# Two PSUM banks of 240 and 280 columns, and one 480-column matmul for the high and the low parts

## The chip, the cores and the metric

The kernel runs on one core of one Trainium2 chip. The metric is the device time of one execution in microseconds (us), given as the median of several runs.

## What is computed

One inference step of a one-layer causal decoder trunk for 512 prompt tokens and 8 sample tokens, D_MODEL 1024, all in float32:

```
z  = rmsnorm(x) @ w_in                       # 1024 x 6656
a_in, b_x, b_gate, c_uv, gates = split(z)
ya = multiscale_pool(a_in)                   # windows 2/4/8/16, per-group 128x128 linear
yb = gelu(b_gate) * rg_lru(conv4(b_x))       # recurrence over the tokens, two 128x128 gates per head
yc = chunk_mlp(gelu(c_uv))                   # rmsnorm(v), triangular mixing in chunks of 128
merged = ga*(ya @ w_pa) + gb*(yb @ w_pb) + gc*(yc @ w_pc)
x  = x + merged @ w_o
x  = x + (gelu(conv3(rmsnorm(x) @ wg)) * (rmsnorm(x) @ wu)) @ wd      # D_FF 3072
y  = final rmsnorm(x)
```

The new states of the pool, the convolutions and the recurrence are outputs too.

## The kernel before

Features lie on the 128 partitions and the 520 tokens along the free axis, so every activation is a set of 128 x 520 tiles. To keep float32 precision with single-pass matmuls, each weight and each activation is split into a high part (rounded to fp32r) and a low part (the rest, also fp32r). The product is wh\*xh + wh\*xl + wl\*xh. For activations `hilo`, `hilos` and `hilo_scaled` (L258 to L277) do this: ScalarE writes the high part, VectorE the low one. For weights `Chunk.high` (L106, ScalarE) and `Chunk.low` (L112, VectorE) do it for each chunk of 128 x 1024 that SP's DMA queue has loaded.

An output tile is a job: 128 output features by 520 tokens, summed over k tiles of 128 input features. Its sums lie in a PSUM tile of two banks, columns 0 to 259 of the tokens in one and 260 to 519 in the other (`TH` = 260). `mm` (L118 to L123) issues six matmuls of 260 columns for each k tile, and each brings its own weight load:

```
ops = ((w[0], x[0]), (w[0], x[1]), (w[1], x[0]))
for n, (ww, xx) in enumerate(ops):
    for h in halves:
        te.matmul(ps[:, h, :TH], ww, xx[:, h * TH:(h + 1) * TH], ...)
```

The jobs have 1184 such k steps in all: 52 tiles of the input projection by 8, 8 each of w_pa and w_pc by 4, 8 each of w_pb and w_o by 8, 24 each of wg and wu by 8, and 16 of wd by 12. `lru` (16 products) and the pool linear (4) call `mm` outside the jobs.

`run_jobs` (L156 to L183) writes the order of all engines by hand. Ahead of a job's matmuls it issues the loads, high parts (`HLEAD` 3) and low parts (`LLEAD` 2) of later chunks. After them comes the job's `post`, which takes the sums from PSUM (on ScalarE for a gelu, a sigmoid or a copy; on VectorE for a product or a sum), and then whatever work was put off to that point (`after`, `chain`). So VectorE's queue holds, for each job: its post, work put off, and the low part of the weight chunk needed two jobs later. There are four PSUM tiles of two banks.

Activations sit in 61 slots (`NA`) of 536 columns. The input `xT` holds 8 of them to the end, since `x1 = xT` is the residual.

At the end, the last two tiles of wd are run half by half, so that the final norm of tokens 0 to 259 (`sums(0)`, `last(0)`) overlaps the matmuls of the other half.

Of the kernel before, what the change touches and what calls it, by code (L numbers as in the profile page):

```python
# [16 lines left out]
P = 128  # L17
# [4 lines left out]
TH = T // 2  # L22
# [24 lines left out]
# columns of the packed states: h0 (j b), conv (j r b), ffn (m r b), pool (g b r)  # L47
# [5 lines left out]
def trunk_kernel(ctx: ExitStack, tc: tile.TileContext, t: dict, o: dict):  # L53
# [9 lines left out]
    def A(name, dt=F32, w=T):  # L63
        return ap_.tile([P, 536], dt, name=name, tag="a", bufs=NA)[:, :w]
# [4 lines left out]
    def acc(ps):  # L69
        return ps[:, :, :TH]  # L70

    def two(x):
        return x.rearrange("p (h c) -> p h c", h=2)
# [4 lines left out]
    # ------------------------------------------------------------------ loads  # L78
# [11 lines left out]
    # ------------------------------------------------------------------ weight chunks  # L90
# [27 lines left out]
    def mm(ps, w, x, first, last, halves=(0, 1)):  # L118
        ops = ((w[0], x[0]), (w[0], x[1]), (w[1], x[0]))
        for n, (ww, xx) in enumerate(ops):  # L120
            for h in halves:
                te.matmul(ps[:, h, :TH], ww, xx[:, h * TH:(h + 1) * TH],  # L122
                          start=first and n == 0, stop=last and n == 2)  # L123
# [26 lines left out]
    def job(parts, post, pre=None, halves=(0, 1), mid=None):  # L150
        """An output tile: parts [(chunk, tile of the chunk, moving operands by k)], and
        post(psum) that takes the sums off; mid = (k, fn) runs fn before that k"""
        jobs.append((parts, post, pre, halves, mid))
        for c, _, _ in parts:
            if c not in order:
                order.append(c)  # L156

    def run_jobs():
        ahead = [(LOADS, "raw", Chunk.load), (HLEAD, "h", Chunk.high), (LLEAD, "l", Chunk.low)]
        at = [0] * 3  # L160
        for n0 in [0, *range(2, len(jobs))]:
# [12 lines left out]
            for n, each in enumerate(zip(*ops)):
                for (c, a, X, k), ps, (_, _, _, halves, mid) in zip(each, pss, group):
                    if mid and mid[0] == n:
                        mid[1]()
                    mm(ps, c.w(k, a), X(k), n == 0, n == len(ops[0]) - 1, halves)
            for ps, each, (_, post, _, halves, _) in zip(pss, ops, group):
                now[0] += len(each) / 8 * len(halves) / 2  # L180
                post(ps)
                run_later(now[0] + 1e-6)
# [8 lines left out]
    # ------------------------------------------------------------------ constants  # L191
# [20 lines left out]
    # state parts of the sample tokens' convolutions  # L212
# [12 lines left out]
    def constants():  # L225
# [8 lines left out]
        # old rows of the sample states  # L234
# [4 lines left out]
    # 4 softplus(-lambda) = 4 (max(-lambda, 0) + log1p(exp(-|lambda|)))  # L239
# [18 lines left out]
    # ------------------------------------------------------------------ helpers  # L258
    def hilo(x, name):
        h, l = A(name + "h", F32R), A(name + "l", F32R)  # L260
        s.activation(h, x, AF.Copy)
        v.tensor_sub(l, x, f(h))
        return h, l

    def hilos(xs, names):
        r = [(A(n + "h", F32R), A(n + "l", F32R)) for n in names]
        for x, (h, _) in zip(xs, r):
            s.activation(h, x, AF.Copy)
        for x, (h, l) in zip(xs, r):
            v.tensor_sub(l, x, f(h))  # L270
        return r

    def hilo_scaled(x, sc_, name):
        h, l = A(name + "h", F32R), A(name + "l", F32R)
        s.activation(h, x, AF.Copy, scale=sc_)
        v.scalar_tensor_tensor(l, x, sc_, f(h), op0=ALU.mult, op1=ALU.subtract)
        return h, l  # L277
# [37 lines left out]
    def rstd_psum(r, name):  # L315
        """[m, n] to all partitions, along the tokens"""
        r, m, tot = r
        ps = PS(name + "b")
        for i, dg in enumerate(r):
            for h in range(tot // TH):  # L320
                te.matmul(ps[:, h, :TH], onesr[:m, :], dg[:, h * TH:(h + 1) * TH], start=i == 0, stop=i == 1)
        return ps

    def rstd_bcast(r, name):
        out = A(name + "r")
        s.activation(two(out), acc(rstd_psum(r, name)), AF.Copy)
# [18 lines left out]
    # ------------------------------------------------------------------ branch B: conv, RG-LRU  # L345
    hs = [None] * 8

    def lru(j, ext):
# [20 lines left out]
        def gates():  # L369
            for n, off in (("r", 0), ("i", 8)):  # L370
# [3 lines left out]
                s.activation(two(y), acc(ps), AF.Sigmoid, bias=pc("bx" if off else "ba", j))  # L374
# [11 lines left out]
        def recip0():  # L386
            v.reciprocal(d["q"][:, :TH], d["q"][:, :TH])

        def recip1():
            v.reciprocal(d["q"][:, TH:], d["q"][:, TH:])  # L390
# [29 lines left out]
    def bx_raw(j, ps):  # L420
        ext = A(f"bx{j}", w=3 + T)
        g.memset(ext[:, :3], 0.0)
        s.activation(two(ext[:, 3:]), acc(ps), AF.Copy)
        held[j] = ext

    def bx_post(j, ps=None):
# [3 lines left out]
        else:  # L430
            ext = A(f"bx{j}", w=3 + T)
            g.memset(ext[:, :3], 0.0)
            v.tensor_mul(two(ext[:, 3:]), acc(ps), two(rs1[0]))
# [26 lines left out]
    # ------------------------------------------------------------------ branch A: pooling  # L460
# [4 lines left out]
    def pool_post(gi, ps):  # L465
# [4 lines left out]
        s.activation(two(a[:, 15:]), acc(ps), AF.Copy)  # L470
# [26 lines left out]
        def out():  # L497
            ps = PS("po")
            mm(ps, c_pw.w(gi), pd[gi], True, True)
            h, l = A(f"ya{gi}h", F32R), A(f"ya{gi}l", F32R)  # L500
            s.activation(two(h), acc(ps), AF.Copy, scale=pc("psc", gi))
            v.scalar_tensor_tensor(two(l), acc(ps), pc("psc", gi), two(f(h)), op0=ALU.mult, op1=ALU.subtract)
            ya[gi] = (h, l)
# [13 lines left out]
    # ------------------------------------------------------------------ gates and merges  # L517
    def gate_jobs(i0, js, gt):
        for j in js:
            def post(ps, j=j):  # L520
                y = A("gt")
                s.activation(two(y), acc(ps), AF.Sigmoid)
# [3 lines left out]
    def merge_jobs(c, i, X, gt, first):  # L526
        for a in range(2):
            def post(ps, j=2 * i + a):
                y = gt.pop(j)
                v.tensor_mul(two(y), acc(ps), two(y))  # L530
# [18 lines left out]
    # ------------------------------------------------------------------ branch C: chunked gating  # L549
# [7 lines left out]
    def v_post(k, ps):  # L557
        vt[k] = A(f"v{k}")
        s.activation(two(vt[k]), acc(ps), AF.Gelu_apprx_tanh)
# [28 lines left out]
    def u_post(k, ps):  # L588
        us[k] = A(f"u{k}")
        s.activation(two(us[k]), acc(ps), AF.Gelu_apprx_tanh)  # L590
# [18 lines left out]
    # ------------------------------------------------------------------ branch B: gate, merge  # L609
# [4 lines left out]
    def bg_post(j, ps):  # L614
        y = A(f"bg{j}")
        s.activation(two(y), acc(ps), AF.Gelu_apprx_tanh)
# [12 lines left out]
    for j in range(8):  # L629
        job([(Chunk(t["w_pb"][j], KD), 0, lambda k: yb[k])], lambda ps, j=j: pb_post(j, ps))  # L630

    # ------------------------------------------------------------------ output projection, norm 2
    xg2 = [None] * 8
    x1 = xT
    st2 = [None]

    def wo_post(j, ps):
        v.tensor_add(two(x1[j]), acc(ps), two(x1[j]))
# [6 lines left out]
    # ------------------------------------------------------------------ channel mixer  # L645
# [5 lines left out]
    def fg_post(m, ps):  # L651
        ext = A(f"fg{m}", w=2 + T)
        g.memset(ext[:, :2], 0.0)
        if rs2[0] is None:
            s.activation(two(ext[:, 2:]), acc(ps), AF.Copy)
            return ext
        v.tensor_mul(two(ext[:, 2:]), acc(ps), two(rs2[0]))
# [29 lines left out]
    def u2_post(m, ps):  # L687
        y = fy.pop(m)
        v.tensor_mul(two(y), acc(ps), two(y))
        hh[m] = hilo(y, f"h{m}_")  # L690

    def dn_post(p, j, ps, halves):
        if len(halves) == 2:
            v.tensor_add(two(x1[j]), acc(ps), two(x1[j]))  # L694
# [7 lines left out]
        c = slice(h * TH, h * TH + TH)  # L702
        v.tensor_add(x1[j][:, c], ps[:, h, :TH], x1[j][:, c])  # L703
# [9 lines left out]
    def sums(h):  # L713
        return rstd_small([st3[0], st3[1]], D, f"n3{h}", h * TH, 4, TH // 4)

    def last(h, r):
        ps = rstd_psum(r, f"n3{h}")
        c = slice(h * TH, h * TH + TH)
        for i, (j0, n) in enumerate(YG):
            y = A(f"y{h}{j0}", w=n * TH).rearrange("p (n c) -> p n c", n=n)  # L720
            for j in range(j0, j0 + n):
                v.scalar_tensor_tensor(y[:, j - j0, :], x1[j][:, c], pc("gf", j), ps[:, 0, :TH],  # L722
# [31 lines left out]
    for k in range(KD):  # L754
        h, l = A(f"xg{k}_h", F32R), A(f"xg{k}_l", F32R)
        s.activation(h, xT[k], AF.Copy, scale=pc("g1", k))  # L756
# [3 lines left out]
        v.scalar_tensor_tensor(l, xT[k], pc("g1", k), f(h), op0=ALU.mult, op1=ALU.subtract)  # L760
# [3 lines left out]
        xg.append((h, l))  # L764
# [5 lines left out]
NA, RAW, HS, LS, LOADS, HLEAD, LLEAD = 61, 4, 5, 4, 3, 3, 2  # L770
# [14 lines left out]
def _layout(w):  # L785
    """The inputs as the launch takes them: the same numbers, laid out by partition."""
# [6 lines left out]
    def cols(a, nk, cw):  # L793
        # (nk * 128, n * cw) -> (n, 128, nk * cw)
# [72 lines left out]
```

## Time and profile before

| | |
|---|---|
| median of 3 runs | 896.65 us (896.6, 896.65, 896.99) |
| span of the profiled execution | 895.0 us |
| PE busy | 884.0 us, 99% |
| VectorE (DVE) busy | 525.2 us, 59% |
| ScalarE (ACT) busy | 344.0 us, 38% |
| HBM read | 82.6 MB |

The span runs from the first to the last instruction of the profiled execution and is 1.65 us under the median of the runs, which also hold what lies around it. PEld is TensorE's weight loads, which overlap the matmuls. Starts in the trace are measured; ends of matmuls are modelled, so distances between starts are what to read.

### The profile page before, as it was taken

How to read it: one execution, taken by the hardware profiler on the slowest of the kernel's cores; microseconds unless marked ns; L12 is line 12 of the kernel's file. 1: busy time of each engine (PE TensorE's matmuls, PEld its weight loads, DVE VectorE, ACT ScalarE, POOL GpSimd, SP SyncE). 2: the span in 40 equal slices, each digit the busy share in tenths (PEclk: the TensorE clock that was granted, in tenths of full speed). 3: DMA queues.
4: the chain of work that ended last, by engine and by line, in shares of the span. 5: the costliest groups of instructions: out<-in, count | busy, mean ns of one | idle time of the engine just before them, and what ended most of it. 6: DMA issues, size and time to landing. Idle time of an engine off the chain costs nothing.

```text
span 895.0 us, 16824 instructions
## 1 busy us (share of the span) xinstructions
PE 884.0 (99%) x7358; PEld 880.8 (98%) x7358; DVE 525.2 (59%) x779; ACT 344.0 (38%) x456; POOL 56.1 (6%) x93
## 2 busy tenths in 40 slices
PE   9999999999999999999999999999999999999995
PEld 8999999999999999999999999999999999999995
DVE  5897998689665442155555666653234555554345
ACT  7554573776342342222334433332122333333210
POOL 1403311111100000000000000000000000000000
PEclk9999999999999999999999999999999999999998
DMA  9423233133232223222321422222332223323212
GB/s 293 152 99 107 73 106 98 57 96 95 72 118 72 94 92 122 71 72 95 95 94 48 131 89 90 88 71 90 106 113 77 95 94 94 95 71 116 74 37 96
DMA packets 28298, 86.12 MB, mean 96 GB/s; under 512 B 3112, under 2 KB 6312, under 8 KB 28200
## 3 DMA queue, kind: packets, MB, share of 16 engines
q1 hardware_dynamic: 26752, 83.21, 29.1%
q10 hardware_dynamic: 1376, 1.44, 0.5%
q8 instruction: 58, 0.95, 0.4%
q0 software_dynamic: 96, 0.39, 0.1%
q14 instruction: 16, 0.13, 0.0%
HBM read 82.63 MB, written 2.79 MB: 95 GB/s over the span
## 4 chain that ended last, share of the span: by engine, by line
PE 98%; DVE 1%; DMA 0%; ACT 0%; issue 0%; DVEq 0%
PE pj L122 95%; PE lru L122 1%; DVE y L722 1%; PE vm L581 0%; DMA par<-in_par 0%; PE po L122 0%; PE vt L574 0%; PE n30p L293 0%; DVE x2q L705 0%; DVE x L703 0%; PE n1p L293 0%; PE nvp L293 0%; PE n2p L293 0%; ACT xg_h L756 0%; PE n31p L293 0%; DVE n L309 0%
## 5 line engine op out<-in xcount | busy, mean ns | idle before, releaser
L112 DVE TENSOR_TENSOR wl<-raw,wh 128x1024 fp32r<-128x1024 f32 (+2 forms) x162 | 182.4, 1136 | 32.5 <-ACT wh L106 32.2
L106 ACT ACTIVATE wh<-raw 128x1024 fp32r<-128x1024 f32 (+2 forms) x162 | 156.7, 975 | 58.5 <-PE pj L122 55.5
L122 PE MATMUL pj<-x_h,wh 128*128 128x260 f32 x768 | 154.6, 283 | 0.0
L122 PE MATMUL pj<-x_h,wl 128*128 128x260 f32 x768 | 154.3, 282 | 0.0
L122 PE MATMUL pj<-x_l,wh 128*128 128x260 f32 x768 | 154.3, 282 | 0.0
L122 PE MATMUL pj<-xn_h,wh 128*128 128x260 f32 x704 | 142.1, 283 | 0.0
L122 PE MATMUL pj<-xn_l,wh 128*128 128x260 f32 x704 | 141.8, 283 | 0.0
L122 PE MATMUL pj<-xn_h,wl 128*128 128x260 f32 x704 | 141.5, 282 | 0.0
L122 PEld LDWEIGHTS pj<-x_h,wl 128*128 128x128 f32 x768 | 118.5, 188 | 0.0
L122 PEld LDWEIGHTS pj<-x_l,wh 128*128 128x128 f32 x768 | 118.1, 188 | 0.0
L122 PEld LDWEIGHTS pj<-x_h,wh 128*128 128x128 f32 x768 | 117.9, 188 | 0.0
L122 PEld LDWEIGHTS pj<-xn_h,wl 128*128 128x128 f32 x704 | 108.5, 188 | 0.0
L122 PEld LDWEIGHTS pj<-xn_h,wh 128*128 128x128 f32 x704 | 108.4, 189 | 0.0
L122 PEld LDWEIGHTS pj<-xn_l,wh 128*128 128x128 f32 x704 | 108.3, 188 | 0.0
L122 PE MATMUL pj<-h_h,wl 128*128 128x260 f32 x384 | 81.3, 283 | 0.0
L122 PE MATMUL pj<-h_h,wh 128*128 128x260 f32 x384 | 81.3, 283 | 0.0
L122 PE MATMUL pj<-h_l,wh 128*128 128x260 f32 x384 | 81.1, 282 | 0.0
L122 PEld LDWEIGHTS pj<-h_h,wl 128*128 128x128 f32 x384 | 60.9, 188 | 0.0
L122 PEld LDWEIGHTS pj<-h_l,wh 128*128 128x128 f32 x384 | 60.8, 188 | 0.0
L122 PEld LDWEIGHTS pj<-h_h,wh 128*128 128x128 f32 x384 | 60.8, 188 | 0.0
L694 DVE TENSOR_TENSOR x<-pj,x 128x520 f32<-128x520 f32 x14 | 9.8, 699 | 77.2 <-PE pj L122 77.2
L665 DVE SCALAR_TENSOR_TENSOR fc<-fg,par,fc 128x512 f32<-128x512 f32 x48 | 36.1, 752 | 18.9 <-ACT fc L663 18.0
(277 smaller groups left out, 1208.7 us busy)
## 6 DMA issues: line engine op xcount, KB each, us to landing
raw<-in_w_in SPq DMA_DIRECT2D x50, 512.0 KB, 3.6
raw<-in_wg SPq DMA_DIRECT2D x24, 512.0 KB, 3.5
raw<-in_wu SPq DMA_DIRECT2D x24, 512.0 KB, 3.5
raw<-in_wd SPq DMA_DIRECT2D x32, 384.0 KB, 3.1
raw<-in_w_pb SPq DMA_DIRECT2D x8, 512.0 KB, 3.5
raw<-in_w_o SPq DMA_DIRECT2D x8, 512.0 KB, 3.6
x<-in_x SPq DMA_DIRECT2D x8, 260.0 KB, 4.6
raw<-in_w_pa SPq DMA_DIRECT2D x4, 512.0 KB, 3.4
```

The source lines that it names most:

```text
L106: s.activation(self.h[:, q], self.raw[:, q], AF.Copy)
L112: v.tensor_sub(self.l[:, q], self.raw[:, q], f(self.h[:, q]))
L122: te.matmul(ps[:, h, :TH], ww, xx[:, h * TH:(h + 1) * TH], start=first and n == 0, stop=last and n == 2)
L665: v.scalar_tensor_tensor(y[:, :SEQ], ext[:, r:r + SEQ], pc("fcw", r * MF + m), y[:, :SEQ], op0=ALU.mult, op1=ALU.add)
L694: v.tensor_add(two(x1[j]), acc(ps), two(x1[j]))
L722: v.scalar_tensor_tensor(y[:, j - j0, :], x1[j][:, c], pc("gf", j), ps[:, 0, :TH], op0=ALU.mult, op1=ALU.mult)
```

## The change

The tokens are cut into 240 (part A) and 280 (part B). The PSUM tile is still two banks: part A ends at the end of bank 0, part B starts at bank 1, so the 520 sums lie side by side. The moving operand of each part is one slot with the low part ahead of the high part (`PAIR`). In a job, for part A, wh is multiplied with both at once: one matmul of 480 columns, whose low half lands in the 240 columns of bank 0 ahead of A's sums. A k step of a job is then five matmuls: 480 (wh; xl and xh of A), 280 (wh, xh of B), 280 (wh, xl of B), 240 (wl, xh of A), 280 (wl, xh of B). Outside the jobs (`lru`, pool) there are still six, of 240 and 280.

After each job that holds part A, `settle` copies the 240 extra columns to SBUF on ScalarE and adds them to A's sums in PSUM on VectorE, ahead of the job's `post`. Every split of an activation is now two instructions on ScalarE and two on VectorE, of 240 and 280 columns. Slots are 57 of 560 columns. `xT` is let go after the first norm; the residual is read again from HBM by 8 DMAs on GpSimd's queue, issued at the fifth tile of w_pb. The last two wd tiles are cut at 240 and 280.

```diff
+TA, TB = 240, 280
+COLS = (slice(0, TA), slice(TA, T))
+    def PAIR(name):
+        r = []
+        for n, w in (("a", TA), ("b", TB)):
+            p = A(name + n, F32R, 2 * w).rearrange("p (i c) -> p i c", i=2)
+            r.append((p[:, 1, :], p[:, 0, :], p))
+        return r
+    def acc(ps, c=slice(0, T)):
+        return ps.rearrange("p h c -> p (h c)")[:, 512 - TA + c.start:512 - TA + c.stop]
+    def mm(ps, w, x, first, last, halves=(0, 1), joint=False):
+        wh, wl = w
+        for h in halves:
+            c = COLS[h]
+            xh, xl, xx = x[h]
+            if h == 0 and joint:
+                te.matmul(ps[:, 0, 512 - 2 * TA:].rearrange("p (i c) -> p i c", i=2), wh, xx,
+                          start=first, stop=False)
+            else:
+                te.matmul(acc(ps, c), wh, xh, start=first, stop=False)
+                te.matmul(acc(ps, c), wh, xl, start=False, stop=False)
+        for h in halves:
+            te.matmul(acc(ps, COLS[h]), wl, x[h][0], start=False, stop=last)
+    def settle(ps):
+        e = ap_.tile([P, TA], F32, name="ex", tag="e", bufs=3)
+        s.activation(e, ps[:, 0, 512 - 2 * TA:512 - TA], AF.Copy)
+        v.tensor_add(acc(ps, COLS[0]), acc(ps, COLS[0]), e)
...
-                    mm(ps, c.w(k, a), X(k), n == 0, n == len(ops[0]) - 1, halves)
+                    mm(ps, c.w(k, a), X(k), n == 0, n == len(ops[0]) - 1, halves, True)
...
+                if 0 in halves:
+                    settle(ps)
                 post(ps)
...
     def hilo(x, name):
-        h, l = A(name + "h", F32R), A(name + "l", F32R)
-        s.activation(h, x, AF.Copy)
-        v.tensor_sub(l, x, f(h))
-        return h, l
+        p = PAIR(name)
+        for c, (h, l, _) in zip(COLS, p):
+            s.activation(h, x[:, c], AF.Copy)
+            v.tensor_sub(l, x[:, c], f(h))
+        return p
...
-    x1 = xT
+    x1 = [None] * 8
+    def reload_x():
+        for j in range(8):
+            x1[j] = A(f"xr{j}")
+            nc.gpsimd.dma_start(x1[j], t["x"][:, j, :])
...
-NA, RAW, HS, LS, LOADS, HLEAD, LLEAD = 61, 4, 5, 4, 3, 3, 2
+SLOT, NA, RAW, HS, LS, LOADS, HLEAD, LLEAD = 2 * TB, 57, 4, 5, 4, 3, 3, 2
+XLOAD = 4
```

## Rows read from the trace of the kernel before

**Rows 1.** The page: engines' shares, and 40 slices of TensorE and its granted clock.

```profile
PE 884.0 (99%) x7358; PEld 880.8 (98%) x7358; DVE 525.2 (59%) x779; ACT 344.0 (38%) x456; POOL 56.1 (6%) x93
...
PE   9999999999999999999999999999999999999995
...
PEclk9999999999999999999999999999999999999998
```

**Rows 2.** The chain that ended last: start us, us, what and how many instructions.

```profile
36.87 34.63 PE pj L122 x288
...
214.16 0.87 PE vt L574 x8
...
227.45 1.78 PE vm L581 x16
...
236.79 236.22 PE pj L122 x1968
```

**Rows 3.** The timeline of TensorE in the first microseconds: start us, us, instructions merged.

```profile
6.51 0.64 PE L122 MATMUL pj<-xg_h,wl 128*128 128x260 f32 x2
6.94 0.61 PE L122 MATMUL pj<-xg_h,wh 128*128 128x260 f32 x2
7.38 0.41 PE L122 MATMUL pj<-xg_l,wh 128*128 128x260 f32 x2
```

**Rows 4.** The timeline of TensorE and its weight loads where 65-column loads follow.

```profile
875.26 0.28 PE L122 MATMUL pj<-h_h,wl 128*128 128x260 f32 x1
875.38 1.06 PE L293 MATMUL n30p<-ones,x2q 128*65 128x1 f32 x16
...
875.26 1.08 PEld L293 LDWEIGHTS n30p<-ones,x2q 128*65 128x65 f32 x16
876.26 0.19 PEld L122 LDWEIGHTS pj<-h_h,wh 128*128 128x128 f32 x1
```

**Rows 5.** Groups by line and shape on VectorE and ScalarE: count, busy us, mean ns.

```profile
L689 DVE TENSOR_TENSOR fc<-pj,fc 128x520 f32<-128x520 f32 x24 | 16.7, 696 | 27.6 <-PE pj L122 27.4
...
L703 DVE TENSOR_TENSOR x<-pj,x 128x260 f32<-128x260 f32 x4 | 1.7, 429 | 4.3 <-PE pj L122 4.3
...
L522 ACT ACTIVATE gt<-pj 128x520 f32<-128x520 f32 x24 | 14.5, 605 | 82.2 <-PE pj L122 78.0 <-issue 4.2
...
L106 ACT ACTIVATE wh<-raw 128x256 fp32r<-128x256 f32 x8 | 2.9, 403 | 0.0
```

**Rows 6.** Busy time of each engine in stretches: us, busy (instructions), PEclk, DMA.

```profile
5.42:17.95 12.53, 12.53 (x96) 12.53 (x97) 10.28 (x18) 9.35 (x16) 0.00 (x0) 1.00 1.00 355
...
36.70:65.60 28.90, 28.90 (x243) 28.90 (x242) 28.07 (x56) 13.69 (x20) 1.99 (x3) 1.00 0.29 95
65.60:162.00 96.40, 96.40 (x805) 96.40 (x804) 82.30 (x116) 48.73 (x66) 24.12 (x22) 1.00 0.30 96
162.00:242.00 80.00, 80.00 (x674) 80.00 (x674) 65.84 (x95) 50.68 (x67) 11.71 (x8) 1.00 0.25 79
242.00:375.00 133.00, 133.00 (x1110) 133.00 (x1109) 56.84 (x70) 46.02 (x58) 0.62 (x1) 1.00 0.32 100
375.00:895.00 520.00, 510.85 (x4276) 510.18 (x4274) 268.39 (x398) 159.49 (x206) 4.13 (x27) 0.99 0.28 88
```

**Rows 7.** VectorE's timeline: low parts of weight chunks, at 64 and 16 us.

```profile
63.15 1.21 DVE L112 TENSOR_TENSOR wl<-raw,wh 128x1024 fp32r<-128x1024 f32 x1
...
15.90 2.49 DVE L112 TENSOR_TENSOR wl<-raw,wh 128x1024 fp32r<-128x1024 f32 x2 [0.84 <-ACT wh L106]
```

**Rows 8.** The chain at the end of the kernel.

```profile
880.80 3.17 DVE y L722 x8
...
889.27 2.38 DVE y L722 x6
```

**Rows 9.** The page's DMA issues: KB each, us from issue to landing.

```profile
x<-in_x SPq DMA_DIRECT2D x8, 260.0 KB, 4.6
```

More of the change, by code (lines that the diff above doesn't have):

```diff
@@ L21 @@
 T = SEQ + NS
-TH = T // 2
+TA, TB = 240, 280
+COLS = (slice(0, TA), slice(TA, T))
 KD = D // P
@@ L63, in A @@
     def A(name, dt=F32, w=T):
-        return ap_.tile([P, 536], dt, name=name, tag="a", bufs=NA)[:, :w]
+        return ap_.tile([P, SLOT], dt, name=name, tag="a", bufs=NA)[:, :w]
     def PS(name):
         return pp.tile([P, 2, 512], F32, name=name, tag="ps")
[L69 to L73, printed above, removed]
+    def PAIR(name):
[6 more added lines that the diff above has]
+        return ps.rearrange("p h c -> p (h c)")[:, 512 - TA + c.start:512 - TA + c.stop]
     def f(x):
@@ L116, in w @@
             return self.h[:, c:c + P], self.l[:, c:c + P]
[L118 to L123, printed above, removed]
+    def mm(ps, w, x, first, last, halves=(0, 1), joint=False):
[15 more added lines that the diff above has]
+        v.tensor_add(acc(ps, COLS[0]), acc(ps, COLS[0]), e)
     now = [0.0]
@@ L259, in hilo @@
     def hilo(x, name):
-        h, l = A(name + "h", F32R), A(name + "l", F32R)
-        s.activation(h, x, AF.Copy)
-        v.tensor_sub(l, x, f(h))
-        return h, l
-    def hilos(xs, names):
[L266 to L270, printed above, removed]
+        p = PAIR(name)
[3 more added lines that the diff above has]
+        return p
+    def hilos(xs, names):
+        r = [PAIR(n) for n in names]
+        for x, p in zip(xs, r):
+            for c, (h, _, _) in zip(COLS, p):
+                s.activation(h, x[:, c], AF.Copy)
+        for x, p in zip(xs, r):
+            for c, (h, l, _) in zip(COLS, p):
+                v.tensor_sub(l, x[:, c], f(h))
         return r
     def hilo_scaled(x, sc_, name):
[L274 to L277, printed above, removed]
+        p = PAIR(name)
+        for c, (h, l, _) in zip(COLS, p):
+            s.activation(h, x[:, c], AF.Copy, scale=sc_)
+            v.scalar_tensor_tensor(l, x[:, c], sc_, f(h), op0=ALU.mult, op1=ALU.subtract)
+        return p
     def square_add(a, x, name):
@@ L319, in rstd_psum @@
         for i, dg in enumerate(r):
-            for h in range(tot // TH):
-                te.matmul(ps[:, h, :TH], onesr[:m, :], dg[:, h * TH:(h + 1) * TH], start=i == 0, stop=i == 1)
+            for c, q in ([(c, c) for c in COLS] if tot == T else [(slice(TA, TA + tot), slice(0, tot))]):
+                te.matmul(acc(ps, c), onesr[:m, :], dg[:, q], start=i == 0, stop=i == 1)
         return ps
@@ L325, in rstd_bcast @@
         out = A(name + "r")
-        s.activation(two(out), acc(rstd_psum(r, name)), AF.Copy)
+        s.activation(out, acc(rstd_psum(r, name)), AF.Copy)
         return out
@@ L373, in gates @@
                 y = A(f"{n}{j}")
-                s.activation(two(y), acc(ps), AF.Sigmoid, bias=pc("bx" if off else "ba", j))
+                s.activation(y, acc(ps), AF.Sigmoid, bias=pc("bx" if off else "ba", j))
                 d[n] = y
@@ L386, in recip0 @@
         def recip0():
-            v.reciprocal(d["q"][:, :TH], d["q"][:, :TH])
+            v.reciprocal(d["q"][:, :TA], d["q"][:, :TA])
         def recip1():
-            v.reciprocal(d["q"][:, TH:], d["q"][:, TH:])
+            v.reciprocal(d["q"][:, TA:], d["q"][:, TA:])
         def coef():
@@ L422, in bx_raw @@
         g.memset(ext[:, :3], 0.0)
-        s.activation(two(ext[:, 3:]), acc(ps), AF.Copy)
+        s.activation(ext[:, 3:], acc(ps), AF.Copy)
         held[j] = ext
@@ L432, in bx_post @@
             g.memset(ext[:, :3], 0.0)
-            v.tensor_mul(two(ext[:, 3:]), acc(ps), two(rs1[0]))
+            v.tensor_mul(ext[:, 3:], acc(ps), rs1[0])
         v.tensor_copy(views["rc"][:, j, :], ext[:, SEQ:])
@@ L469, in pool_post @@
         g.memset(a[:, :15], 0.0)
-        s.activation(two(a[:, 15:]), acc(ps), AF.Copy)
+        s.activation(a[:, 15:], acc(ps), AF.Copy)
         x = A(f"pd{gi}")
@@ L499, in out @@
             mm(ps, c_pw.w(gi), pd[gi], True, True)
[L500 to L503, printed above, removed]
+            ya[gi] = hilo_scaled(acc(ps), pc("psc", gi), f"ya{gi}")
         chain(1, [sums, means, split, None, out])
@@ L521, in post @@
                 y = A("gt")
-                s.activation(two(y), acc(ps), AF.Sigmoid)
+                s.activation(y, acc(ps), AF.Sigmoid)
                 gt[j] = y
@@ L529, in post @@
                 y = gt.pop(j)
-                v.tensor_mul(two(y), acc(ps), two(y))
+                v.tensor_mul(y, acc(ps), y)
                 if first:
@@ L558, in v_post @@
         vt[k] = A(f"v{k}")
-        s.activation(two(vt[k]), acc(ps), AF.Gelu_apprx_tanh)
+        s.activation(vt[k], acc(ps), AF.Gelu_apprx_tanh)
         vst[0] = square_add(vst[0], vt[k], f"vq{k}")
@@ L589, in u_post @@
         us[k] = A(f"u{k}")
-        s.activation(two(us[k]), acc(ps), AF.Gelu_apprx_tanh)
+        s.activation(us[k], acc(ps), AF.Gelu_apprx_tanh)
     def yc_split(k):
@@ L615, in bg_post @@
         y = A(f"bg{j}")
-        s.activation(two(y), acc(ps), AF.Gelu_apprx_tanh)
+        s.activation(y, acc(ps), AF.Gelu_apprx_tanh)
         v.tensor_mul(y, y, hs[j])
@@ L621, in pb_post @@
         y = gb[j]
-        v.tensor_mul(two(y), acc(ps), two(y))
+        v.tensor_mul(y, acc(ps), y)
         v.tensor_add(y, y, merged[j])
@@ L629, in trunk_kernel @@
     for j in range(8):
-        job([(Chunk(t["w_pb"][j], KD), 0, lambda k: yb[k])], lambda ps, j=j: pb_post(j, ps))
+        job([(Chunk(t["w_pb"][j], KD), 0, lambda k: yb[k])], lambda ps, j=j: pb_post(j, ps), (lambda: reload_x()) if j == XLOAD else None)
     xg2 = [None] * 8
-    x1 = xT
+    x1 = [None] * 8
     st2 = [None]
+    def reload_x():
+        for j in range(8):
+            x1[j] = A(f"xr{j}")
+            nc.gpsimd.dma_start(x1[j], t["x"][:, j, :])
     def wo_post(j, ps):
-        v.tensor_add(two(x1[j]), acc(ps), two(x1[j]))
+        v.tensor_add(x1[j], acc(ps), x1[j])
         xg2[j] = hilo_scaled(x1[j], pc("g2", j), f"x1{j}_")
@@ L654, in fg_post @@
         if rs2[0] is None:
-            s.activation(two(ext[:, 2:]), acc(ps), AF.Copy)
+            s.activation(ext[:, 2:], acc(ps), AF.Copy)
             return ext
-        v.tensor_mul(two(ext[:, 2:]), acc(ps), two(rs2[0]))
+        v.tensor_mul(ext[:, 2:], acc(ps), rs2[0])
         fg_rest(m, ext)
@@ L688, in u2_post @@
         y = fy.pop(m)
-        v.tensor_mul(two(y), acc(ps), two(y))
+        v.tensor_mul(y, acc(ps), y)
         hh[m] = hilo(y, f"h{m}_")
@@ L693, in dn_post @@
         if len(halves) == 2:
-            v.tensor_add(two(x1[j]), acc(ps), two(x1[j]))
+            v.tensor_add(x1[j], acc(ps), x1[j])
             if p == 1:
@@ L701, in dn_post @@
         h = halves[0]
-        c = slice(h * TH, h * TH + TH)
-        v.tensor_add(x1[j][:, c], ps[:, h, :TH], x1[j][:, c])
+        c = COLS[h]
+        v.tensor_add(x1[j][:, c], acc(ps, c), x1[j][:, c])
         q = A(f"x2q{j}{h}")
@@ L713, in sums @@
     def sums(h):
-        return rstd_small([st3[0], st3[1]], D, f"n3{h}", h * TH, 4, TH // 4)
+        return rstd_small([st3[0], st3[1]], D, f"n3{h}", COLS[h].start, 4, (TA, TB)[h] // 4)
     def last(h, r):
         ps = rstd_psum(r, f"n3{h}")
-        c = slice(h * TH, h * TH + TH)
+        c, m = COLS[h], (TA, TB)[h]
         for i, (j0, n) in enumerate(YG):
-            y = A(f"y{h}{j0}", w=n * TH).rearrange("p (n c) -> p n c", n=n)
+            y = A(f"y{h}{j0}", w=n * m).rearrange("p (n c) -> p n c", n=n)
             for j in range(j0, j0 + n):
-                v.scalar_tensor_tensor(y[:, j - j0, :], x1[j][:, c], pc("gf", j), ps[:, 0, :TH],
+                v.scalar_tensor_tensor(y[:, j - j0, :], x1[j][:, c], pc("gf", j), acc(ps, slice(TA, TA + m)),
                                        op0=ALU.mult, op1=ALU.mult)
@@ L754, in trunk_kernel @@
     for k in range(KD):
-        h, l = A(f"xg{k}_h", F32R), A(f"xg{k}_l", F32R)
-        s.activation(h, xT[k], AF.Copy, scale=pc("g1", k))
+        p = PAIR(f"xg{k}")
+        for c, (h, _, _) in zip(COLS, p):
+            s.activation(h, xT[k][:, c], AF.Copy, scale=pc("g1", k))
         if k % 2 == 0:
@@ L759, in trunk_kernel @@
                 c.high((k, k + 2))
-        v.scalar_tensor_tensor(l, xT[k], pc("g1", k), f(h), op0=ALU.mult, op1=ALU.subtract)
+        for c, (h, l, _) in zip(COLS, p):
+            v.scalar_tensor_tensor(l, xT[k][:, c], pc("g1", k), f(h), op0=ALU.mult, op1=ALU.subtract)
         if k % 2 == 0:
@@ L763, in trunk_kernel @@
                 c.low((k, k + 2))
-        xg.append((h, l))
+        xg.append(p)
     after(1, constants)
```

## The prediction

> **What bounds the kernel now.** I read the page first, then the chain that ended last, then starts in the timeline, then the other engines stretch by stretch. TensorE is busy for 884.0 of 895.0 us, in every slice but the last, at the upper clock level (2.4 GHz) from start to end [rows 1]. The chain is made of matmuls alone in long pieces: 1968 of them in 236.22 us without one wait, so a matmul of 260 columns takes 120.0 ns [rows 2]. 260 columns at 2.4 GHz are 108.3 ns. So 11.7 ns of each matmul are not columns, and a k step of six is 720.0 ns, of which 650 are columns and 70 are not. Only what shortens this step, or makes TensorE wait, can move the end.
>
> What the 11.7 ns are decides the change, and three readings can be told apart in part. (a) A fixed cost of each matmul. (b) A slower rate per column. (c) Slack: the load of the next weights needs 120 ns, or the stream is padded to that length, and columns up to there cost nothing. Against (c) as a load speaks the place where 65-column loads follow: the last 260-column matmul starts at 875.26, the next matmul at 875.38, 0.12 us later as everywhere, though its load is short: the sixteen loads of 65 columns start within 1.00 us, the first 0.12 us ahead of the rest, so some 59 ns each [rows 4]. The moving stream, not the next load, holds these 120 ns. Before 7.4 us two matmuls take 0.43 to 0.44 us, 0.217 us each, which is 260 columns at the lower level of 1.2 GHz with nothing on top [rows 3]; what needs 120 ns is hidden there, as any of the three would be. Between (a) and (b) rows hardly decide: float32 passes of 128 columns take 0.87/8 = 109 and 1.78/16 = 111 ns [rows 2], another type at another rate.
>
> VectorE is at 59% on average [rows 1], but not everywhere: 28.07 of 28.9 us from 36.7 to 65.6, 82.3 of 96.4 to 162, 65.8 of 80 to 242, and near half after that [rows 6]. In the first of these it is late: a low weight part is done at 63.15 + 1.21 = 64.36 [rows 7], and the tile that reads it begins at 36.87 + 5/6 of 34.63 = 65.7 [rows 2], a margin of 1.4 us.
>
> **The change part by part.**
>
> *Five matmuls for six.* The columns stay: 480 + 3 x 280 + 240 = 1560 = 6 x 260. Under (a) a step is 1560/2.4 + 5 x 11.7 = 708.3 ns: 480 takes 211.7, 280 takes 128.3, 240 takes 111.7. That is 11.7 ns less in each of the 1184 steps: 13.9 us. Lower bound, (b): nothing. Upper bound, (c): 480 at 200 and four at 120 are 680 ns, 40 less, 47.4 us. I take 13.9, since the row nearest to the question [rows 4] excludes the load, and a bubble per matmul needs no other assumption. The 20 products outside the jobs keep six matmuls and 1560 columns: nothing.
>
> The Trainium skill has a rule here that speaks against the change: "TensorE: Matmul & The Clock Gate", section "Wait — 56ns, not 53.3ns?", gives a fixed cost of about 2.5 ns for a matmul at 2.4 GHz, whatever its width. The rows show 11.7 beyond the columns, so the trace does not agree that 2.5 is all; if only that much were fixed and the rest went with the columns, the step would save 2.5 ns and the kernel 3.0 us (an estimate from that page).
>
> *settle.* 148 tiles pay one copy and one add. ScalarE's copy of 240 columns from PSUM: 605 ns for 520 and 403 for 256 [rows 5] give 0.77 ns a column, so 0.39 us. VectorE's add: 429 ns for 260 and 696 for 520 [rows 5], 1.03 ns a column, so 0.41 us. No row shows an add that writes to PSUM: between 0.41 and the 0.70 of a full tile; I take 0.41, nearest in size. 61 us more on VectorE, 58 on ScalarE. The `post` starts 0.8 us later; where the next reader is a whole tile away this is hidden by that tile's 5.7 us. The tightest is w_o's last tile, read by wg's first tile at its eighth k step, 7 x 0.708 = 5.0 us later; its add, high part and low part, at 0.6 to 0.7 us each for 520 columns [rows 5], take some 2.1 us before and 3.3 after, with settle and split. Hidden; if not, about 1 us at each of two such joints.
>
> *Splits in two.* An operation of 520 in two of about 260: 2 x 429 - 696 = 0.16 us on VectorE for each of 84 splits; on ScalarE 2 x 403 - 605 = 0.20.
>
> *Where that cover is thin.* From 36.7 to 65.6 five tiles bring 5 x 0.41 and the eight splits of xn and one of bc 9 x 0.16: 3.5 us, against 0.8 us idle [rows 6] and a margin of 1.4 us: 1.3 us of stall, and TensorE would also be 0.5 us faster there, which it can't use: 1.8 us. What is late is the low weight part, queued behind the new add. From 65.6 to 162 there are 19 evacuations (eight of them of half tiles in k) and some 15 splits: 10.2 us more in 14.1 us of idle [rows 6]. On average it fits, piece by piece not always: 1.5 us. From 162 to 242, 12 evacuations and 6 splits, 5.9 in 14.2: 0.5 us. After that VectorE goes from 52% to some 60%: nothing.
>
> *Start.* The first 480-column matmul needs the low part too, and ScalarE's two half splits are 0.1 to 0.2 longer; VectorE carries eight more halves, 1.3 us, in a stretch where it is busy for 10.28 of 12.53 [rows 6] and where the third tile's low part came about 0.8 us ahead of use (the first of two ending at 15.90 + 1.25 = 17.1, tile at 17.95) [rows 6, 7]: 1.0 us.
>
> *End.* Part B's norm works on 280 columns instead of 260: its eight products, 2.38/6 = 0.40 us each, grow by 20 x 1.03 ns = 0.02, the sums a little: 0.3 us. Part A's eight, 3.17 us ahead of that [rows 8], shrink by as much, off the path.
>
> *Slots and the second read of x.* Four slots less while xT lives, four more (57 against 61 - 8 = 53) after it: nothing, unless the first 65 us need the four, where late splits would cost the same stall again, 0 to 2 us. The 8 DMAs of 260 KB land in 4.6 us each [rows 9], on a queue with nothing else to do there, some 20 us ahead of the first use, at a mean DMA load of 0.28 [rows 6]: nothing.
>
> *Sum.* -13.9 + 1.8 + 1.5 + 0.5 + 1.0 + 0.3 = -8.8 us. On the span 895.0 that is 886.2; with the 1.65 us between span and median, **888 us**. 0.2%, 1.8 us, is about what a measurement of this kernel can tell from no change.
>
> **The rivals.**
>
> *Slack (c), or a stream padded in larger pieces.* For it: 120 ns is the same at every stage [rows 2]. Against: [rows 4] for the load. Full, it gives 47.4 us; the 24 tiles up to 162 us, where VectorE has no more room, keep little of their 24 x 0.32 = 7.7, and the stalls of 5.1 stay: about -34, 862. Half of it (a step of 692 to 694) gives -20 to -24: 872 to 876. Chance 0.22.
>
> *Columns pay (b).* The saving is 0, or 2.7 if the 109 ns of [rows 2] are 128 columns at 0.83 and 2.3 fixed (1184 x 2.3); the stalls of 5.1 stay: 899 to 902. For it: the passes at 1.2 GHz show no fixed cost [rows 3]. The rule of the Trainium skill weighed above ("TensorE: Matmul & The Clock Gate") would lead here. Chance 0.14.
>
> *VectorE becomes the bound (the other side).* Place: the add stands at the head of VectorE's queue until ScalarE has copied the same tile, so a tile may cost it 0.41 + 0.39 = 0.80, or 0.70 + 0.39 = 1.09. In the 24 evacuations from 36.7 to 162, idle time and margin are 0.8 + 14.1 + 1.4 = 16.3 us and the splits take 3.8. The gain of 13.9 is gone when an evacuation costs (16.3 - 3.8 + 13.9)/24 = 1.1 us. At 0.80 the stall is 6.7 more than nothing, so 891; above 1.1 slower, 898 to 908. Against it: where VectorE is late, the copy is long done. Chance of the slower part 0.10.
>
> *Narrow passes are slower.* No fp32r pass under 260 columns is in the trace. At the 111/128 = 0.87 ns a column of the float32 passes [rows 2], 240 columns take 209 ns, 97 more a step: above 1000 us. Chance 0.04.
>
> **How the numbers follow.** The forecast as summed has 0.50, with its own range of 882 to 897 (stalls from 1 to 14 us). Together: faster by over 0.2% is 0.46 of the forecast, the 0.22 of slack and 0.02 of the rest, 0.70; same 0.09 from the ends of the forecast and of (b); slower 0.21. The range 855 to 903 leaves out the far end of slack, the far end of VectorE's case and the narrow passes, some 0.15.
>
> **What would show it.** After: in the long pieces, starts 0.212 us after a 480-column matmul, 0.128 after 280, 0.112 after 240, a tile of 48 replaced by one of 40 in 5.67 us. 0.20 and 0.12 would be slack; 0.2215, 0.129, 0.111 would be columns. Waits of TensorE on VectorE's low weight parts, between 36 and 70 us above all, of 2 to 5 us in sum, would show the stall. The prediction is wrong if the step does not change, if it falls by far more than 12 ns, or if waits on VectorE exceed 10 us.

## The result and the profile after

The changed kernel takes 925.76 us against 896.62 of the kernel before on the same chip: ratio 1.0324, 95% interval 1.031 to 1.0339. The forecast of 888 us was wrong in sign; the time lies beyond the range too.

The page of the changed kernel: TensorE is no longer fully busy in every slice, and its granted clock falls in some.

```profile
span 923.6 us, 14942 instructions
...
PE 890.4 (96%) x6174; PEld 848.3 (92%) x6174; DVE 591.4 (64%) x1011; ACT 399.2 (43%) x688; POOL 58.3 (6%) x101
...
PE   9999899879899999999999999999999999999995
...
PEclk9999999998899999999999999999999999999998
...
L145 DVE TENSOR_TENSOR pj<-pj,ex 128x240 f32<-128x240 f32 x148 | 61.1, 413 | 202.4 <-ACT ex L144 202.4
...
L144 ACT ACTIVATE ex<-pj 128x240 f32<-128x240 f32 x148 | 54.2, 366 | 252.9 <-PE pj L140 252.5
```

settle's two operations take about what was worked out, 0.41 us on VectorE and 0.37 on ScalarE for each of 148 tiles. Against [rows 1] TensorE has 1184 instructions less, and yet 6.4 us more busy time. Set against the kernel before at equal progress (k steps of the jobs, by the starts of their matmuls), the changed kernel is 1.2 us late after 48 k steps, 7.9 after 144, 13.8 after 192, 24.6 after 240 and 31.3 after 288, at 268 us. Over the 864 steps from there to step 1152 it wins 3.3 us back. So there are two things to explain: 30 us lost before 270 us, and a gain of some 4 ns a step where 11.7 were forecast.

Stretches of the changed kernel (us, busy and instructions of PE, PEld, DVE, ACT, POOL, then granted clock), to be read against [rows 6]:

```profile
36.00:262.00 226.00, 204.56 (x1381) 194.31 (x1382) 183.41 (x324) 123.69 (x210) 37.15 (x39) 0.95 0.25 79
196.00:204.00 8.00, 6.11 (x43) 5.60 (x41) 3.96 (x6) 7.07 (x10) 1.52 (x1) 1.00 0.22 66
204.00:214.00 10.00, 5.56 (x24) 5.35 (x25) 8.63 (x13) 4.44 (x9) 1.53 (x1) 0.51 0.23 59
...
262.00:900.00 638.00, 637.76 (x4462) 611.11 (x4461) 372.00 (x606) 248.65 (x426) 7.95 (x34) 1.00 0.30 93
```

From 36 to 262 us TensorE stands still for 21.4 us. VectorE has more to do than before, but it is not saturated. The k steps from 48 to 288, in the kernel before and in the changed one:

```profile
42.48:236.55 194.07, 194.07 (x1625) 194.07 (x1623) 165.50 (x240) 109.80 (x148) 37.83 (x33) 1.00 0.29 94
```

```profile
43.68:267.80 224.12, 203.72 (x1383) 193.74 (x1383) 181.28 (x300) 123.06 (x209) 36.68 (x34) 0.95 0.26 81
```

VectorE has 15.8 us more work in the same k steps and takes 30.1 us longer; it is busy for 81% of that time, where it was 85%. Who waited for whom between 36 and 262 us (us in total, times, longest), TensorE first, then ScalarE:

```profile
PE nvp L321 <- DVE vq L312: 6.3, 1, 6.3
PE vt L599 <- ACT gt L547: 4.5, 1, 4.5
PE pj L134 <- DVE gt L555: 3.0, 1, 3.0
PE pj L134 <- ACT a L498: 2.5, 1, 2.5
PE pj L140 <- DVE wl L121: 1.9, 3, 1.3
...
ACT gt L547 <- DVE pj L145: 22.6, 10, 4.8
...
ACT v L584 <- DVE pj L145: 11.8, 3, 4.9
ACT a L498 <- DVE pj L145: 10.4, 4, 5.5
...
ACT u L615 <- DVE pj L145: 7.1, 3, 3.1
```

The low weight part (wl), which the prediction named as what would be late, is a small part of it (1.9 us). Three of TensorE's lines, 10.0 us in sum, name a post (gt, a) that has nothing to give it: there TensorE needs one of the four PSUM tiles, and the post that would empty it is late. ScalarE's posts (gt, v, a, u) wait for settle's add, 52 us in sum. The longest stall, in the timelines of ScalarE, VectorE and TensorE of the changed kernel:

```profile
195.46 0.60 ACT L584 ACTIVATE v<-pj 128x520 f32<-128x520 f32 x1 [4.85 <-DVE pj L145]
...
201.49 0.36 ACT L144 ACTIVATE ex<-pj 128x240 f32<-128x240 f32 x1
...
206.38 0.60 ACT L584 ACTIVATE v<-pj 128x520 f32<-128x520 f32 x1 [3.23 <-DVE pj L145]
207.02 0.64 ACT L309 ACTIVATE vq<-v 128x520 f32<-128x520 f32 x1
```

```profile
200.67 2.33 DVE L384 SCALAR_TENSOR_TENSOR bc<-bx,par,bc 128x512 f32<-128x512 f32 x3 [3.21 <-ACT bc L382]
...
203.05 1.90 DVE L418 RECIPROCAL q<-q 128x280 f32<-128x280 f32 x1
204.87 1.16 DVE L121 TENSOR_TENSOR wl<-raw,wh 128x1024 fp32r<-128x1024 f32 x1
205.94 0.41 DVE L145 TENSOR_TENSOR pj<-pj,ex 128x240 f32<-128x240 f32 x1
207.69 0.70 DVE L312 TENSOR_TENSOR vq<-vq,vq 128x520 f32<-128x520 f32 x1 [1.34 <-ACT vq L309]
```

```profile
208.44 1.89 PE L321 MATMUL nvp<-ones,vq 128*104 128x1 f32 x10 [6.33 <-DVE vq L312]
210.19 0.75 PE L134 MATMUL pj<-xn_a,wh 128*128 128x480 f32 x1
210.74 0.43 PE L137 MATMUL pj<-xn_b,wh 128*128 128x280 f32 x1
```

The copy is done at 201.85. VectorE reaches the add only at 205.94, behind a reciprocal and a weight part that the gelu has no need of. The gelu of v waits 3.23 us for the add, its square follows, VectorE then waits for that square, and TensorE, whose queue holds the sums of squares (nvp) at this point, stands still for 6.33 us.

Why VectorE came so late stands in the first lines. ScalarE's gelu of the tile before had waited 4.85 us for settle's add, so the work behind it in ScalarE's queue was late, and VectorE stood still for 3.21 us until ScalarE had written bc (L382). So the two queues hold each other up in turn.

The granted clock is 0.51 from 204 to 214 us: the lower level of 1.2 GHz. It fell 2 us into the 6.33 us without work and rose 6 us after TensorE had work again, and the matmuls in between go at about half speed (280 columns took 0.23 us from start to start, against 0.129 at the upper level). From 36 to 262 us there are four such stretches (from 98.4, 170.1, 204.2 and 241.7 us); the longest, and the sum of the four:

```profile
204.19:214.43 10.24, 5.99 (x26) 5.78 (x27) 8.87 (x13) 4.87 (x9) 1.53 (x1) 0.50 0.24 59
...
sum 23.89, PE 17.44 PEld 16.67 DVE 20.44 ACT 12.20 POOL 1.53; mean PE 4.36 PEld 4.17 DVE 5.11 ACT 3.05 POOL 0.38
```

At 0.129 for 0.233 us, the 17.4 us of matmuls in them would have taken some 8 us less at the upper level (an estimate). With the 21.4 us of standing still that is some 29 us, about all of the loss.

### The profile page after: what moved, and what is told of

Same layout as the page of the kernel before. It is cut to its first block, busy times and chain, and to the rows that moved or that the text cites. A ratio compares the mean times of both kernels' runs of the same rounds, so it can differ in the third digit from the quotient of the medians.

```text
span 923.6 us, 14942 instructions
## 1 busy us (share of the span) xinstructions
PE 890.4 (96%) x6174; PEld 848.3 (92%) x6174; DVE 591.4 (64%) x1011; ACT 399.2 (43%) x688; POOL 58.3 (6%) x101
## 4 chain that ended last, share of the span: by engine, by line
PE 72%; DVE 19%; ACT 6%; DMA 1%; issue 1%; DVEq 0%; ACTq 0%
PE pj L140 24%; PE pj L134 22%; PE pj L137 13%; PE pj L138 13%; DVE wl L121 3%; DVE bc L384 2%; DVE pj L145 1%; DVE q L415 1%; DVE h L437 1%; DVE xs L370 1%; DVE q L418 1%; DVE xq L312 1%; DVE gt L555 1%; DMA raw<-in_w_in 1%; DMA x<-in_x 0%
## 5 line engine op out<-in xcount | busy, mean ns | idle before, releaser
L134 PE MATMUL pj<-x_a,wh 128*128 128x480 f32 x384 | 145.7, 379 | 0.0
L134 PE MATMUL pj<-xn_a,wh 128*128 128x480 f32 x352 | 137.4, 390 | 5.5 <-DVE gt L555 3.0
L140 PE MATMUL pj<-x_b,wl 128*128 128x280 f32 x384 | 112.5, 293 | 0.0
L137 PE MATMUL pj<-x_b,wh 128*128 128x280 f32 x384 | 111.8, 291 | 0.0
L138 PE MATMUL pj<-x_b,wh 128*128 128x280 f32 x384 | 111.4, 290 | 0.0
L140 PE MATMUL pj<-x_a,wl 128*128 128x240 f32 x384 | 104.8, 273 | 0.2 <-DVE wl L121 0.2
L140 PE MATMUL pj<-xn_b,wl 128*128 128x280 f32 x352 | 104.7, 298 | 0.0
L137 PE MATMUL pj<-xn_b,wh 128*128 128x280 f32 x352 | 104.0, 295 | 0.0
L138 PE MATMUL pj<-xn_b,wh 128*128 128x280 f32 x352 | 103.5, 294 | 0.0
L140 PE MATMUL pj<-xn_a,wl 128*128 128x240 f32 x352 | 97.6, 277 | 1.5 <-DVE wl L121 1.5
L138 PEld LDWEIGHTS pj<-x_b,wh 128*128 128x128 f32 x384 | 72.0, 187 | 11.3
L134 PEld LDWEIGHTS pj<-x_a,wh 128*128 128x128 f32 x384 | 72.6, 189 | 0.0
L137 PEld LDWEIGHTS pj<-x_b,wh 128*128 128x128 f32 x384 | 72.1, 188 | 0.0
```

The lines of the kernel that those rows point to most:

```text
L134: te.matmul(ps[:, 0, 512 - 2 * TA:].rearrange("p (i c) -> p i c", i=2), wh, xx, start=first, stop=False)
L137: te.matmul(acc(ps, c), wh, xh, start=first, stop=False)
L138: te.matmul(acc(ps, c), wh, xl, start=False, stop=False)
L140: te.matmul(acc(ps, COLS[h]), wl, x[h][0], start=False, stop=last)
```

## Experiments

The theory then (S): settle chains VectorE and ScalarE behind each other at the end of every tile, where its sums are taken out of PSUM (the evacuation). Rivals: the doubled splits and the fewer slots (D); the new operand layout or the wide matmul itself (M).

**Six matmuls, no settle** (e1):

```diff
-                    mm(ps, c.w(k, a), X(k), n == 0, n == len(ops[0]) - 1, halves, True)
+                    mm(ps, c.w(k, a), X(k), n == 0, n == len(ops[0]) - 1, halves, False)
-                if 0 in halves:
-                    settle(ps)
```

> The changed kernel without the 480-column matmul and without settle: in the jobs six matmuls a k step again (three of 240, three of 280), everything else as changed (splits in two, 57 slots, second read of x). Theory S (settle chains VectorE and ScalarE behind each other at every tile's end, and TensorE waits for what is queued behind): 896 to 901 us, TensorE waits under 3 us before 270 us, granted clock 0.99 or more. Theory D (the doubled splits and fewer slots make VectorE and ScalarE late): 915 us or more, with most of the 22 us of waits still there. Theory M (the new operand layout is slow to stream): a k step clearly over 720 ns.

Measured: 901.54 us, ratio 1.0052 (1.0037 to 1.0068), clock 0.996, no wait of TensorE over 1.5 us. D falls. At step 288 it is 0.5 us behind the kernel before, so splits and slots cost next to nothing up to there (the second read of x comes later). The rest of the loss grows evenly over the 895 steps after it, some 4 to 5 ns a step: a dearer step, which speaks for M, in small.

**The wide matmul, no settle** (e2): only the two settle lines taken out, so the sums lack one product.

> The changed kernel with the 480-column matmul but without settle; the wh*xl product of part A is left out of the sums. Theory S: no waits beyond those of before, a k step of 714 ns, so 896.6 - 1184 x 6 ns = 889.5, with a little for the splits 889 to 893 us. Theory D: 910 us or more. If a 480-column matmul itself cost what the change lost, 920 or more.

Measured: 893.91 us, ratio 0.9971 (0.9959 to 0.9982). TensorE is busy all the way:

```profile
36.00:262.00 226.00, 226.00 (x1615) 217.60 (x1614) 195.88 (x322) 126.77 (x194) 38.30 (x36) 1.00 0.30 92
```

settle costs 925.76 - 893.91 = 31.9 us, and one matmul less in a step is worth 901.54 - 893.91 = 7.6 us, 6.4 ns a step, against six matmuls of the same cut. Theory S stands; the gain expected on the kernel before was too high (889.5, a band of 889 to 893).

**Wide matmul and settle only late, or only early** (e4, e5): the last argument of `mm` and the condition of settle become `n0 >= 52`, or `n0 < 52`.

> The changed kernel with the 480-column matmul and settle only in the jobs from the gelu gate tiles of branch B on (job 52), six matmuls and no settle ahead of them. From there 804 of the 1184 k steps are joint. Theory S: the stretch to 280 us as before, then 804 x 4 ns = 3 us won (the changed kernel gained 3.3 us in 864 steps there): 892 to 896 us. Theory D: 915 or more.

Measured: 895.49 us, ratio 0.999 (0.9981 to 0.9998). The jobs from 52 on hold 832 k steps by the trace, not 804.

> The counterpart: 480-column matmul and settle only in jobs 0 to 51, six matmuls after them. Theory S: the whole loss of 31 us stays and the late gain of 3.3 us is gone: 927 to 931 us, with the reduced granted clock between 100 and 260 us. Theory D: about the same as the run with six matmuls everywhere.

Measured: 933.25 us, ratio 1.0407 (1.0388 to 1.0426), clock 0.981. The loss was 33.2 us at step 288, 2 more than expected and than in the changed kernel, of which 3.5 stood at step 48 already (the changed kernel: 1.2). Its trace shows a stretch at the lower clock level from 39.3 us on, 3.4 us full of matmuls, that the changed kernel's trace has not; by the estimate above that is 1.5 us. Place and cause are settled: settle, in the first 52 jobs.

What in settle? Three readings: the hop (H: VectorE stands until ScalarE has copied), the place (P: every evacuation now goes through VectorE's queue, so ScalarE's posts stand behind whatever is in it), the work (W: 61 us more on VectorE).

**VectorE copies and adds** (e3): `s.activation(e, ...)` becomes `v.tensor_copy(e, ...)`.

> settle done by VectorE alone: it copies the 240 extra columns to SBUF and adds them, two operations of 0.41 us, with nothing of it on ScalarE. Theory H (the price is the hop: VectorE stands still until ScalarE's copy of the same tile is done): clearly under 925, some 905 to 915. Theory P (the price is that every evacuation now goes through VectorE's late queue, so ScalarE's post stands behind it): 930 or more, as VectorE gets 61 us more. Theory W (VectorE's added work alone): 940 or more.

Measured: 945.45 us, ratio 1.0544 (1.0528 to 1.0559). H would have gained; it lost 19.7 more. It does not part P from W.

**ScalarE's copy alone** (e7): the add is left out.

> settle without the add: ScalarE still copies the 240 columns, VectorE does nothing, so the low part of A is left out of the sums. All three theories: near the run without settle (893.9), 894 to 898; if ScalarE's 54 us of copies were the price, 910 or more.

Measured: 894.4 us, ratio 0.9975 (0.9965 to 0.9984). 54 us on ScalarE, and its wait for the tile's end, cost 0.5 us.

**VectorE's add alone, in its place** (e8):

```diff
-        e = ap_.tile([P, TA], F32, name="ex", tag="e", bufs=3)
-        s.activation(e, ps[:, 0, 512 - 2 * TA:512 - TA], AF.Copy)
-        v.tensor_add(acc(ps, COLS[0]), acc(ps, COLS[0]), e)
+        v.tensor_scalar_add(acc(ps, COLS[0]), acc(ps, COLS[0]), 0.0)
```

> settle without ScalarE's copy: VectorE adds 0 to part A's sums in PSUM, an operation of the same size at the same place ahead of the post; the low part of A is left out. Theory H: 894 to 900, since VectorE waits for nobody. Theory P: 912 or more, most of the loss, since ScalarE's posts still stand behind VectorE. Theory W: 912 or more.

Measured: 922.46 us, ratio 1.0282 (1.0267 to 1.0297). Without the hop nearly all of the loss is there, with the same longest waits of TensorE:

```profile
PE nvp L319 <- DVE vq L310: 6.3, 1, 6.3
PE vt L597 <- ACT gt L545: 4.5, 1, 4.5
PE pj L134 <- DVE gt L553: 3.0, 1, 3.0
```

```profile
36.00:262.00 226.00, 204.84 (x1404) 194.93 (x1403) 184.61 (x322) 112.87 (x174) 36.84 (x35) 0.96 0.25 79
```

TensorE stands still for 21.2 us in this stretch, as in the changed kernel (21.4). The 3.3 us between the two runs are not more standing: the changed kernel's trace has 23.9 us at the lower clock level there, this one 17.1.

**The same work, out of the evacuation** (e9): at settle's place `v.tensor_add(e, fill, fill)`, 240 columns between SBUF tiles of its own (two buffers for e instead of three, to make room for fill).

> VectorE's work of settle without its place in the evacuation: an add of 240 columns between SBUF tiles of its own, in VectorE's queue where settle's add was, that nobody waits for; the low part of A is left out. Theory H and theory P: 894 to 900. Theory W: 912 or more.

Measured: 900.67 us, ratio 1.0046 (1.0031 to 1.006). Its stretch from 36 to 262 us:

```profile
36.00:262.00 226.00, 220.99 (x1564) 212.14 (x1563) 204.81 (x354) 124.56 (x192) 38.56 (x36) 0.99 0.29 88
```

VectorE gets through more work than in the changed kernel (204.8 against 183.4) and TensorE stands for 5.0 us instead of 21.4. The work costs 900.67 - 893.91 = 6.8 us, just past the band of 894 to 900 and far from W's 912; its place in the evacuation 922.46 - 900.67 = 21.8; the hop 925.76 - 922.46 = 3.3. Theory P is the main one; W and H have their shares.

One thing the 21.8 us do not part. In the evacuation the add makes ScalarE's post wait for VectorE, and it also makes VectorE wait for the tile's last matmul, where the post is not its own. e9's add waits for nobody. In e8 VectorE's longest waits between 36 and 262 us were

```profile
DVE bc L382 <- ACT bc L380: 12.3, 5, 3.6
DVE bc_a L285 <- ACT bc_a L284: 10.3, 5, 6.0
DVE pj L143 <- PE pj L140: 6.8, 3, 3.9
```

The tile's end held VectorE for 6.8 us, ScalarE's work for 22.6 (the same two waits took 11.7 in e9). Both had grown, so some of the 21.8 us may be VectorE held to the tile's end; no run tests that alone.

**Only where the post is VectorE's own** (e11): the condition is `n0 in VJOBS`, 19 early jobs.

```diff
+VJOBS = {5, 6, 7, *range(20, 28), 42, 43, *range(46, 52)}
```

> Joint matmul and settle only in 19 early jobs whose post is VectorE's own (jobs 5 to 7 of the recurrent branch, the merges of w_pa and w_pc), six matmuls in all other jobs, early and late. Compare with six everywhere, 901.5. Theory P (the loss comes from ScalarE's posts standing behind VectorE): 901 to 905, for 19 adds of 0.41 us and 88 joint steps. If settle costs the same wherever VectorE is loaded (31 us over 56 early jobs): 909 to 913.

Measured: 905.75 us, ratio 1.01 (1.0086 to 1.0113): 4.2 us over six everywhere. It lies just past P's band and below the other. In the mean such a tile costs 0.22 us, against 0.6 for the 52 early jobs at large (32 us). But the trace shows no price for each tile: from 36 to 262 us TensorE has one wait,

```profile
PE pj L137 <- DVE gt L555: 2.5, 1, 2.5
```

and soon after it 3.4 us at the lower clock level, some 1.5 us by the estimate above. Together that is 4.0 of the 4.2 us. In e9 the same wait (2.8 us) is the longest. That fits P: where the post is VectorE's own, what is left is close to the price of the added work.

**What the cut costs** (e12): six matmuls, cut at 260 and 260, the rest as changed.

```diff
-TA, TB = 240, 280
+TA, TB = 260, 260
```

> Six matmuls, no settle, cut at 260 and 260, the rest as changed (splits in two, 57 slots, second read of x). If the 4.8 us of the 240/280 six-matmul run come from the unequal cut: 896.5 to 898 and a step of 720. If from the doubled splits and the slots: 900 to 902.

Measured: 896.05 us, ratio 0.9992 (0.9983 to 1.0001), no change, and 0.45 us under the band of the first reading. So two halves for each split, 57 slots and the second read of x cost nothing that can be measured, and the 4.8 us of e1 (901.54) are the unequal cut.

**The late version cut at 256 and 264** (e10): `TA, TB = 256, 264`, slots of 536 columns, otherwise e4.

> As the run with the joint matmul only from job 52 on, but cut at 256 and 264 columns (joint matmul 512 wide, slots of 536). Theory C (a matmul costs its columns at 0.46 ns, only the wide joint one a little less): a k step of six at 720 again instead of 724, the tail 16 columns shorter: 1.2 us less early, 0.3 at the end, so 892.5 to 895. Theory F (a fixed cost per matmul, with 240 and 280 as good as any): the same as the 240/280 version, 895.5.

Measured: 895.74 us, ratio 0.9987 (0.9978 to 0.9996), the same as e4 within their intervals. The time is the one that F gave and lies 0.7 us above C's band. But C's band ended only half a microsecond below F's value, too little for the time to decide what a matmul costs; the starts below do. No version that computes the whole product beats the kernel before by more than 1.2 us; e2, which leaves a product out, is 2.8 us under it, and with this cut that bounds what a cheaper settle could bring.

**The step itself.** The timeline of TensorE in the changed kernel where nothing waits, one k step and the start of the next:

```profile
700.22 0.38 PE L134 MATMUL pj<-h_a,wh 128*128 128x480 f32 x1
700.43 0.29 PE L137 MATMUL pj<-h_b,wh 128*128 128x280 f32 x1
700.56 0.29 PE L138 MATMUL pj<-h_b,wh 128*128 128x280 f32 x1
700.68 0.27 PE L140 MATMUL pj<-h_a,wl 128*128 128x240 f32 x1
700.80 0.29 PE L140 MATMUL pj<-h_b,wl 128*128 128x280 f32 x1
700.92 0.39 PE L134 MATMUL pj<-h_a,wh 128*128 128x480 f32 x1
```

Mean distances between starts from 520 to 850 us, at the upper clock level:

| columns | kernel | mean ns | ns a column |
|---|---|---|---|
| 240 | changed | 110.4 | 0.460 |
| 256 | e10 | 117.4 | 0.459 |
| 260 | before | 119.8 | 0.461 |
| 264 | e10 | 122.1 | 0.462 |
| 280 | changed | 129.0 | 0.461 |
| 480 | changed | 217.6 | 0.453 |
| 512 | e10 | 231.9 | 0.453 |

From 240 to 480 the slope is (217.6 - 110.4)/240 = 0.447 ns a column, which leaves 3.2 ns fixed; 256 and 512 fit this to 0.2 ns, 260 to 280 lie up to 1.0 above. By the same working e2 and e4 give 0.449 and 0.447 ns a column with 1.9 and 2.3 ns fixed, and e10, from 256 to 512, 0.447 with 2.9. So the fixed part is 2 to 3 ns, and the columns are the rest. The step is 217.6 + 3 x 129.0 + 110.4 = 715 ns, against 6 x 119.8 = 719 before and 3 x (111.1 + 129.9) = 723 in e1; in e2, from start to start of the steps, it is 716.5.

## Why the prediction was wrong, point by point

- **"Five matmuls for six"** took all 11.7 ns beyond 2.4 GHz as a fixed cost of a matmul: 13.9 us. This term was mis-sized. Measured: 2 to 3 ns fixed, the rest goes with the columns. The step fell by 2 to 4 ns, not 11.7, and without settle (e2) the kernel wins 2.8 us. This is the rival (b), "columns pay", given 0.14. Of the starts that the prediction named as its test, those of 280 and 240 columns (0.129 and 0.110 us) are too near under both readings to tell; 480 columns took 0.2176 us, between its 0.212 for a fixed cost and its 0.2215 for columns. The Trainium skill's rule weighed there ("TensorE: Matmul & The Clock Gate", section "Wait — 56ns, not 53.3ns?", about 2.5 ns fixed) was the better guide to the fixed part: 1.9 to 3.2 measured. Its other half, 1/2.4 ns a column, is not what these fp32r matmuls show (0.447). That the load was not the limit, from [rows 4], held: 240 columns, each matmul with a load of its own, pass in 110.4.
- **"settle", "The post starts 0.8 us later; where the next reader is a whole tile away this is hidden".** This step failed, and with it the sign. The delay is not 0.8 us but the length of whatever is ahead in VectorE's queue, 4.1 us in the case shown, and what is ahead there may itself be waiting for ScalarE. ScalarE's posts, which had needed nobody but TensorE, now wait for that queue, and what they put off is not hidden: TensorE waited for sums of squares and for PSUM tiles that late posts had not emptied. Its waits on VectorE alone are over 10 us (6.3, 3.0 and 1.9 among them), one of the prediction's own signs of being wrong. The 21.8 us between e9 and e8 are this, with what VectorE's wait for the tile's end adds.
- **"Where that cover is thin"** weighed VectorE's added work against its idle time and came to 3.8 us. The work alone costs 6.8 us (e9): undersized, not the cause. A sum of busy time can't see an order: VectorE's busy share even fell.
- **"What is late is the low weight part".** Mostly not: it was 1.9 us of the waits; sums of squares, and transposes and tiles behind late evacuations, were most of the rest.
- **"VectorE becomes the bound"**, the rival of the other side, had the place and the sign, 0.10. Its mechanism was the hop (3.3 us), and its price a budget of VectorE's time. "Where VectorE is late, the copy is long done" was true in the case shown, and beside the point.
- **The clock** was left out. The stalls bring stretches at the lower level; with none (e2, e12) the clock is 0.995 or more, in e3 0.975. It was not measured by itself; from the trace of the changed kernel it is some 8 of the 32 us.
- **"Start", 1.0 us:** no run shows it. At step 32 the changed kernel was 0.6 us ahead of the kernel before, and e2 was 0.1 ahead at step 48.
- **Right:** splits after the start, slots, the second read of x (e12); the end, 0.2 us longer (last matmul of a job to the end of the span: 11.3 before, 11.5 after), where 0.3 was forecast.

## What to carry to other kernels

An operation put ahead of an evacuation moves that evacuation into the queue of its engine: price it at what stands ahead in that queue, and follow who reads next: small matmuls in TensorE's own queue, and whoever needs the PSUM tile. Busy shares mislead here: VectorE's share fell from 85% to 81% with more work to do, the sign of two queues that wait for each other. Before buying fewer, wider matmuls, look for two widths in the trace: one width can't part a fixed cost from a cost per column.

## What was not expected of the hardware

An fp32r matmul cost 0.447 ns a column, 7% over 1/2.4 ns, plus 2 to 3 ns, for widths of 240 to 512, each with a weight load of its own. Six matmuls of 240 and 280 are 4 ns a step dearer than six of 260 (723 against 719), for the same columns; the reason stays open. The 6.33 us without work on TensorE came with 10.2 us at the lower clock level, 6 of them after the work was back.
